# Second feed-forward product of an encoder layer: 26 block products on 4x4x2 blocks in place of one Strassen level

## The chip, the cores and the metric

One Trainium2 chip, one core. The metric is the device time of one execution in microseconds (us). The five engines that the text names are TensorE (PE), VectorE (DVE), ScalarE (ACT), GpSimd (POOL) and SyncE (SP). Here POOL and SP do little but issue transfers (DMA).

## The reference

One layer of a bidirectional encoder on x of 1024 tokens by 1024 channels. The first half (a gated mixing branch, a windowed attention branch, their merge) is untouched by the change. The second half is

```python
h2 = rmsnorm(x, norm2_g) * (1.0 + sc2) + sh2          # sc2, sh2, gt2: columns of silu(c) @ w_ada + b_ada
f_gate, f_up = jnp.split(h2 @ w_ffn_in, 2, axis=-1)   # w_ffn_in: 1024 x 5632
x = x + gt2 * ((jax.nn.silu(f_gate) * f_up) @ w_ffn_out)   # w_ffn_out: 2816 x 1024
```

All is fp32. The first feed-forward product is `h2 @ w_ffn_in`; the second is the hidden matrix (1024 tokens by 2816) times `w_ffn_out`.

## The kernel before

**Precision.** A matrix operand is split in two fp32r halves (`split2`: ACT casts it to the high half, DVE subtracts the high half from the value and writes the low half). A product of two operands is three matmuls: high by high, high by low, low by high.

**First feed-forward product.** The 2816 hidden columns are 22 tiles of 128, f = 0 to 21, in one level of Strassen: seven half-size products (STEPS, i = 0 to 6) of 12 matmuls for each f. The order is written out by hand: under `manual_schedule` each engine executes what is in the code, in the order in which it is in the code, and waits on semaphores. For f = 2 to 5 only i = 2 to 6 stand in the main loop (i = 0 and 1 came earlier); from f = 6 on all seven stand there. In one pass of the loop, `product(f, i)` issues the matmuls, `prepare(u + 2, 1)` works two weight units ahead (sums of weight blocks `ws` on DVE, cast on ACT, low half `wl` on DVE), and `evict(f, i)` combines the product in `xs`, `hs`, `t` or `t2`, applies silu on ACT and at i = 6 writes two tiles `hid` (minus the hidden values) of 128 x 512. PE waits for a low half if that is late.

**Sums for the second product.** `hidden_sums` forms four sums of hidden blocks for two f, one DVE operation a pass (`run_later`), and POOL stores the blocks in `tA`, `tB`; `load_out` loads `w_ffn_out` from f = 6 on, `out_sums` forms four weight sums and POOL stores them in `wS`.

**Second feed-forward product.** `work` has 77 units (seven Strassen products by 11 pairs of K tiles). A unit is [128 x 1024]: 512 columns of weights, 512 tokens of hidden values. SP loads it 12 units ahead in two transfers (`fetch`), `split_step` splits it four ahead, PE does 12 matmuls (`step_mm`). Units 0 to 2 use buffers of the first product's pool; the loads of later units wait until PE has read the last operand of the first product. Results are evicted by `finish`, `finish_rest` and `second_row` into accumulators `c1`, `e4`, `e7` and rows of x reloaded from DRAM (`x1d`). Within this stage eight columns of the gate gt2 are computed: SP loads 512 KB of `w_ada` and `ada_late` multiplies and reduces them in one DVE operation, written by the program as `raw<-raw,mid`. The last product's last row is done in two halves of 256 tokens.

All compute instructions carry the line of one helper (L144 before, L224 after); `dma` (SP) and `pool_dma` (POOL) are helpers too (L1265 and L1262).

Of the kernel before, what the change touches and what calls it, by code (L numbers as in the profile page):

```python
# [106 lines left out]
def kernel(  # L107
# [1816 lines left out]
    def hidden_tiles(f):  # L1924
        e, t = divmod(f, 2)
        if e not in hidden:
            hidden[e] = [mid.tile([P, 2048], F32, tag="mid", name=nm("hid"))]
        o = hidden[e][0]
        return [o[:, i * Q : (i + 1) * Q] for i in (2 * t, 2 * t + 1)]
# [29 lines left out]
    later = []  # L1959

    def run_later(n):
        for _ in range(n):
            if later:
                later.pop(0)()

    def hidden_sums(f):

        e, t = divmod(f, 2)
        if t == 0:
            hidden[e].append(mid.tile([P, 2048], F32, tag="mid", name=nm("hid")))  # L1970
        o, n = hidden[e]
        b = [o[:, i * Q : (i + 1) * Q] for i in range(4)]
        d = [n[:, i * Q : (i + 1) * Q] for i in range(4)]
        if t == 0:
            later.append(lambda: V.tensor_tensor(d[0], b[0], b[1], op=ALU.subtract))
            return
        pool_dma(tA[e], o)
        later.append(lambda: V.scalar_tensor_tensor(out=d[1], in0=d[0], scalar=-1.0, in1=b[3],
                                                    op0=ALU.mult, op1=ALU.subtract))
        later.append(lambda: V.tensor_tensor(d[2], b[3], b[1], op=ALU.subtract))  # L1980
        later.append(lambda: (V.scalar_tensor_tensor(out=d[3], in0=d[1], scalar=-1.0, in1=b[2],
                                                     op0=ALU.mult, op1=ALU.subtract),
                              pool_dma(tB[e], n)))

    wo_raw = {}

    def load_out(e):
        wo_raw[e] = mid.tile([P, 2048], F32, tag="mid", name=nm("wo"))
        for t in range(2):
            pool_dma(wo_raw[e][:, t * UNIT : (t + 1) * UNIT], w_out[2 * e + t])  # L1990

    def out_sums(e, part):

        w = wo_raw[e]
        a11, a21, a12, a22 = (w[:, i * Q : (i + 1) * Q] for i in range(4))
        out, a, b = ((a22, a21, a22), (a21, a11, a21), (a11, a22, a11), (a12, a11, a12))[part]
        V.tensor_tensor(out, a, b, op=ALU.add)
        if part == 3:
            pool_dma(wS[e], w)


# [90 lines left out]
    def out_row(e, t, d):  # L2092
        return w_out[2 * e + t][:, d * Q : (d + 1) * Q]

    def blk(x, i):
        return lambda e: x[e][:, i * Q : (i + 1) * Q]


    OUT = (
        (lambda e: out_row(e, 0, 0), blk(tA, 0), 1, True),  # L2100
        (lambda e: out_row(e, 1, 0), blk(tA, 2), 1, False),
        (blk(wS, 1), blk(tB, 2), 0, True),
        (lambda e: out_row(e, 1, 1), blk(tB, 3), 0, False),
        (blk(wS, 3), blk(tB, 0), 1, True),
        (blk(wS, 0), blk(tB, 1), 1, False),
        (blk(wS, 2), blk(tA, 3), 1, False),
    )
# [304 lines left out]
```

## Time and profile before

| | |
|---|---|
| median of 3 runs | 1211.98 us (1211.6 to 1212.04) |
| profiled execution | 1211.91 us, of which the span is 1210.1 us |
| PE busy | 1203.6 us (99%), 5632 matmuls |
| DVE busy | 924.0 us (76%) |
| ACT busy | 584.8 us (48%) |
| POOL busy | 155.4 us (13%) |
| DMA | 243.10 MB, mean 201 GB/s |
| first feed-forward product, main loop f = 2 to 5 | 637.50 to 691.91 us |
| f = 6 to 21 | 691.91 to 996.89 us |
| second feed-forward product | 996.89 us to the end |

Rows of the trace give start and duration in us, the engine, the operation and `out<-in` by tile names; a bracket at the end is the idle time before it and what ended it. The chain of waits is followed back from the last instruction, so engines on it set the end. DVE durations overlap a little at their ends: start to start of two neighbours is the pace. "us to landing" of a DMA counts from its issue to the arrival of its data.

### The profile page before, as it was taken

How to read it: one execution, taken by the hardware profiler on the slowest of the kernel's cores; microseconds unless marked ns; L12 is line 12 of the kernel's file. 1: busy time of each engine (PE TensorE's matmuls, PEld its weight loads, DVE VectorE, ACT ScalarE, POOL GpSimd, SP SyncE). 2: the span in 40 equal slices, each digit the busy share in tenths (PEclk: the TensorE clock that was granted, in tenths of full speed). 3: DMA queues.
4: the chain of work that ended last, by engine and by line, in shares of the span. 5: the costliest groups of instructions: out<-in, count | busy, mean ns of one | idle time of the engine just before them, and what ended most of it. 6: DMA issues, size and time to landing. Idle time of an engine off the chain costs nothing.

```text
span 1210.1 us, 15610 instructions
## 1 busy us (share of the span) xinstructions
PE 1203.6 (99%) x5632; PEld 1004.1 (83%) x5632; DVE 924.0 (76%) x1496; ACT 584.8 (48%) x958; POOL 155.4 (13%) x190
## 2 busy tenths in 40 slices
PE   9999999999999999999999999999999999999998
PEld 7888888888888888888888888888888888888887
DVE  9999967889978876898987757676676665765646
ACT  6668845367855443745553333333333334433341
POOL 0124323114322000011000000000000000000001
PEclk9999999999999999999999999999999999999999
DMA  9745169753177643567313545454555449995552
GB/s 372 283 157 192 35 228 318 289 226 122 71 273 266 213 150 100 172 222 266 104 61 118 187 175 208 182 201 158 181 207 191 157 168 380 393 344 191 193 173 105
DMA packets 80285, 243.10 MB, mean 201 GB/s; under 512 B 9168, under 2 KB 9424, under 8 KB 74960
## 3 DMA queue, kind: packets, MB, share of 16 engines
q1 hardware_dynamic: 64576, 167.65, 39.8%
q0 software_dynamic: 15632, 74.46, 16.2%
q8 instruction: 44, 0.72, 0.2%
q14 instruction: 33, 0.27, 0.1%
HBM read 180.73 MB, written 61.34 MB: 200 GB/s over the span
## 4 chain that ended last, share of the span: by engine, by line
PE 96%; DVE 2%; ACT 1%; DMA 0%; issue 0%; SPq 0%; DVEq 0%; ACTq 0%
PE mm L144 49%; PE at L144 47%; DVE mid L144 1%; ACT mid L144 0%; DVE wl L144 0%; DMA mid<-in_xA_dram 0%; DVE h L144 0%; ACT wh L144 0%; DVE lb L144 0%; ACT qhl L144 0%; DVE qhl L144 0%; ACT h L144 0%; DVE t L144 0%; SPq L201 0%; ACT kbuf L144 0%
## 5 line engine op out<-in xcount | busy, mean ns | idle before, releaser
L144 ACT CAST wh<-raw 128x1024 fp32r<-128x1024 f32 (+1 forms) x154 | 157.3, 1022 | 120.1 <-PE mm L144 39.5
L144 DVE TENSOR_TENSOR wl<-raw,wh 128x1024 fp32r<-128x1024 f32 (+1 forms) x141 | 165.2, 1175 | 61.4 <-ACT wh L144 60.5
L144 PE MATMUL mm<-mid,wh 128*128 128x512 f32 x640 | 197.3, 389 | 0.0
L144 PEld LDWEIGHTS mm<-mid,wh 128*128 128x128 f32 x640 | 119.9, 188 | 24.8
L144 PE MATMUL mm<-wh,h 128*128 128x512 f32 x384 | 124.6, 396 | 0.2 <-ACT h L144 0.2
L144 PE MATMUL mm<-mid,wl 128*128 128x512 f32 x320 | 124.5, 389 | 0.0
L144 PE MATMUL mm<-h,wh 128*128 128x512 f32 x304 | 94.3, 391 | 0.0
L144 PE MATMUL at<-h,wh 128*128 128x512 f32 x304 | 93.8, 390 | 0.0
L144 PEld LDWEIGHTS mm<-wh,h 128*128 128x128 f32 x384 | 70.7, 188 | 13.8 <-ACT h L144 0.4
L144 DVE TENSOR_TENSOR wl<-ws,wh 128x1024 fp32r<-128x1024 f32 (+1 forms) x50 | 55.9, 1117 | 24.4 <-ACT wh L144 24.4
L144 PE MATMUL mm<-wl,h 128*128 128x512 f32 x192 | 71.2, 391 | 0.0
L144 PEld LDWEIGHTS mm<-mid,wl 128*128 128x128 f32 x320 | 60.1, 188 | 12.4
L144 PEld LDWEIGHTS at<-h,wh 128*128 128x128 f32 x304 | 56.9, 188 | 11.7
L144 ACT CAST wh<-ws 128x1024 fp32r<-128x1024 f32 (+1 forms) x50 | 48.3, 966 | 37.3 <-DVE ws L144 24.9
L144 PEld LDWEIGHTS mm<-h,wh 128*128 128x128 f32 x304 | 56.6, 188 | 11.6
L144 ACT ACTIVATE t<-t 128x512 f32<-128x512 f32 x46 | 28.4, 630 | 70.8 <-DVE t L144 70.8
L144 DVE TENSOR_TENSOR ol<-raw,oh 128x1024 fp32r<-128x1024 f32 x30 | 36.6, 1223 | 31.1 <-ACT oh L144 29.4
L144 PE MATMUL at<-h,wl 128*128 128x512 f32 x152 | 59.3, 390 | 0.0
L144 PE MATMUL mm<-h,wl 128*128 128x512 f32 x152 | 59.2, 389 | 0.0
L144 ACT ACTIVATE xs<-xs 128x512 f32<-128x512 f32 x21 | 13.3, 632 | 94.0 <-DVE xs L144 94.0
L144 ACT CAST oh<-raw 128x1024 fp32r<-128x1024 f32 x30 | 31.7, 1055 | 44.4 <-PE at L144 21.6
L144 PE MATMUL at<-wl,wh 128*128 128x512 f32 (+1 forms) x136 | 52.7, 388 | 0.0
(302 smaller groups left out, 2871.0 us busy)
## 6 DMA issues: line engine op xcount, KB each, us to landing
mid<-in_w_ada_dram SPq DMA_DIRECT2D x30, 512.0 KB, 8.1
raw<-in_w_gate_dram SPq DMA_DIRECT2D x26, 512.0 KB, 3.8
tA<-hid POOLq DMA_DIRECT2D x11, 1024.0 KB, 4.6
tB<-hid POOLq DMA_DIRECT2D x11, 1024.0 KB, 5.2
wo<-in_w_out_dram POOLq DMA_DIRECT2D x22, 512.0 KB, 6.0
wS<-wo POOLq DMA_DIRECT2D x11, 1024.0 KB, 5.1
raw<-wS SPq DMA_DIRECT2D x44, 256.0 KB, 3.2
raw<-tB SPq DMA_DIRECT2D x44, 256.0 KB, 5.0
```

Of the source, the lines that this page charges most:

```text
L144: ins = f(*args, **kw)
```

## The change

The second product on the first 20 K tiles (five groups g of four tiles) uses 26 products of blocks (4 blocks of 256 weight columns, 4 K tiles, 2 halves of the tokens) where the plain product has 32; tiles 20 and 21 are done plainly (8 tail products). Each of the 130 units (26 products by 5 groups) is [128 x 768], 256 columns of weights and 512 tokens, with 6 matmuls; a tail product has 12.

- **Weight sums (A).** 28 sums of weight blocks (`A_OPS`), for two, two and one groups at a time: 84 DVE operations. Operands are loaded by SP in five registers of 128 x 512 (four in a tile `sums`, one `ss`) by a plan made by `registers`; results go by POOL to `pU` or `aX`, some come back later. 78 loads, 66 stores.
- **Token sums (B).** 18 sums of hidden blocks for each group: 90 DVE operations on eight registers (`hid` and the second `sums` tile), 14 loads and 18 stores a group. A group starts at f = 6, 8, 12, 16, 20. `evict` now stores the hidden tiles (`hR`, `hT`).
- **Place.** `run_sums(RATE)` issues 1.4 sums a pass from f = 2 on, in f = 2 to 5 all of them A.
- **gt2.** The eight `ada_late` and their loads (one buffer of 512 KB, in the second `sums` tile) move from the second product to the passes s = 0, 2, ... 16 of f = 2 to 5.
- **Second product.** `ORDER` gives the order of products, the bank pair and, for each result, the output rows and sign; DVE adds it straight to the row of x. A unit is split five ahead.
- **Removed.** `hidden_sums`, `out_sums`, `load_out`, `tA`, `tB`, `wS`, and the accumulators.

The diff, cut:

```diff
+NG = 5
+TAIL = 4 * NG
+UCOL = 768
+AHEAD_OF = 5
+RATE = 1.4
+A_OPS = (
+    (16, 0, 4, 1, -1), (17, 16, 2, 1, -1), (18, 17, 4, 1, 1), (19, 10, 2, -1, -1), (20, 11, 10, 1, -1),
...
+B_OPS = (
+    (8, 2, 6, 1, -1), (9, 3, 8, -1, 1), (10, 6, 9, 1, 1), (11, 0, 2, 1, 1), (12, 7, 9, 1, 1),
...
+    A_PLAN, B_PLAN = registers(A_ALL, 5, 3), registers(B_OPS, 8, 3)
...
+    def a_step(k):
+        (batch, v), _, _, ca, cb = A_ALL[k]
+        o, a, b = A_PLAN[1][k]
+        dst, n = a_place((batch, v))
+        w = slice(0, n * 256)
+        combine(a_regs[o][:, w], a_regs[a][:, w], a_regs[b][:, w], ca, cb)
+        if slot_of(A_OF, v) or (batch, v) in a_later:
+            pool_dma(dst, view(a_regs[o], dst, n))
+        a_loads(k)
...
+    def b_step(g, k):
+        v, _, _, ca, cb = B_OPS[k]
+        o, a, b = B_PLAN[1][k]
+        combine(b_regs[o], b_regs[a], b_regs[b], ca, cb)
+        for p in slot_of(B_OF, v):
+            pool_dma(pU[p, g][:, 256:], b_regs[o])
+        b_loads(g, k)
...
+    def gt2_step(n):
+        cond, raw = (gt2["m"][:, i * UNIT : (i + 1) * UNIT] for i in range(2))
+        if n > 0:
+            ada_late(raw, GT2 + n - 1, cond)
+        if n < 8:
+            dma(raw, w_ada2[GT2 - GT1 + n])
...
-            if i == 6:
-                hidden_sums(f)
-            elif f > 2:
-                run_later(1)
...
+                if s < 18 and s % 2 == 0:
+                    gt2_step(s // 2)
+                if i == 0 and f in (6, 8, 12, 16, 20):
+                    g = f // 4 - 1
+                    while b_queue:
+                        b_step(*b_queue.pop(0))
+                    b_loads(g, -1)
+                    b_queue.extend((g, k) for k in range(len(B_OPS)))
+                elif s:
+                    run_sums(RATE, 34 + 28 * max(0, (s - 6) // 28) - s)
...
-        for n in range(2, 4):
+        for n in range(2, AHEAD_OF):
             split_step(n)
...
+        def evict_out(k, x, sign, d, bank, cs=slice(0, Q)):
...
+            V.scalar_tensor_tensor(out=o, in0=bank[:, : cs.stop - cs.start], scalar=gt, in1=o,
+                                   op0=ALU.mult, op1=ALU.add)
```

**How DVE's order moves.** Three places, in DVE's program order. At the turn from f = 2 to f = 3, before (the two rows with `hid_1133` on the left are hidden sums):

```order
L144 TENSOR_TENSOR wl_1145_6309<-ws_1072_5753,wh_1144_6308 128x1024
L144 TENSOR_TENSOR wl_1151_6333<-ru_5754,wh_1150_6332 128x512
L144 TENSOR_TENSOR hid_1133_6203<-hid_1118_6062 128x512
L144 SCALAR_TENSOR_TENSOR hid_1133_6203<-hid_1133_6203,hid_1118_6062 128x512
L144 TENSOR_TENSOR ws_1072_5753<-ws_1072_5753 128x512
L144 TENSOR_TENSOR ws_1072_5753<-ws_1072_5753,raw_1130_6179 128x512
```

and now; a row that writes `sums_1140` or `ss_1141` is a weight sum, a row that writes `sums_1139,acc_mod_96` is one `ada_late`:

```order
L224 TENSOR_TENSOR wl_1147_6333<-ws_1072_5754,wh_1146_6332 128x1024
L224 SCALAR_TENSOR_TENSOR sums_1139_6249,acc_mod_96<-sums_1139_6249 128x1024
L224 TENSOR_TENSOR sums_1140_6250<-sums_1140_6250 128x512
L224 TENSOR_TENSOR wl_1151_6362<-ru_5755,wh_1150_6361 128x512
L224 SCALAR_TENSOR_TENSOR sums_1140_6250<-sums_1140_6250 128x512
L224 SCALAR_TENSOR_TENSOR sums_1139_6249,acc_mod_96<-sums_1139_6249 128x1024
L224 SCALAR_TENSOR_TENSOR sums_1140_6250<-sums_1140_6250 128x512
L224 TENSOR_TENSOR sums_1140_6250<-ss_1141_6251,sums_1140_6250 128x512
L224 TENSOR_TENSOR ws_1072_5754<-ws_1072_5754 128x512
L224 TENSOR_TENSOR ws_1072_5754<-ws_1072_5754,raw_1130_6180 128x512
```

Between the low half of a unit and the weight sums `ws` of the next one, two of the eight `ada_late` and four weight sums take the place of two hidden sums; between the two `ada_late` stand three operations.

The end of f = 5 and the start of f = 6, from the eviction of (5, 4) to the low half that the third product of f = 6 reads, before:

```order
L144 TENSOR_TENSOR xs_1175_6542<-mm_1108_5982,xs_1175_6542 128x512
L144 TENSOR_TENSOR wl_1177_6557<-raw_1147_6315,wh_1176_6556 128x1024
L144 TENSOR_TENSOR xs_1171_6521<-at_1174_6529,xs_1171_6521 128x512
L144 TENSOR_TENSOR ws_1072_5753<-ws_1072_5753 128x512
L144 TENSOR_TENSOR ws_1072_5753<-ws_1072_5753,raw_1147_6315 128x512
L144 SCALAR_TENSOR_TENSOR hid_1168_6502<-xs_1175_6542,xs_1171_6521 128x512
L144 SCALAR_TENSOR_TENSOR hid_1168_6502<-mm_1108_5982,hs_1109_5998 128x512
L144 TENSOR_TENSOR wl_1179_6590<-ws_1072_5753,wh_1178_6589 128x1024
```

and now:

```order
L224 TENSOR_TENSOR xs_1173_6611<-mm_1108_5983,xs_1173_6611 128x512
L224 TENSOR_TENSOR wl_1175_6635<-raw_1148_6340,wh_1174_6634 128x1024
L224 TENSOR_TENSOR sums_1140_6250<-sums_1140_6250 128x512
L224 TENSOR_TENSOR xs_1169_6587<-at_1172_6598,xs_1169_6587 128x512
L224 TENSOR_TENSOR sums_1140_6250<-sums_1140_6250 128x512 x2
L224 TENSOR_TENSOR ws_1072_5754<-ws_1072_5754 128x512
L224 TENSOR_TENSOR ws_1072_5754<-ws_1072_5754,raw_1148_6340 128x512
L224 SCALAR_TENSOR_TENSOR hid_1118_6063<-xs_1173_6611,xs_1169_6587 128x512
L224 SCALAR_TENSOR_TENSOR hid_1118_6063<-mm_1108_5983,hs_1109_5999 128x512
L224 TENSOR_TENSOR wl_1177_6675<-ws_1072_5754,wh_1176_6674 128x1024
```

Three weight sums (one row stands for two) came in between, ahead of the low half; the other added operations of f = 2 to 5 stand ahead of the first row shown.

The turn to the second product, from the low half of unit 0 on (`raw_1404` before, `raw_1378` now), before:

```order
L144 TENSOR_TENSOR wl_1444_8676<-raw_1404_8358,wh_1443_8675 128x1024
L144 TENSOR_TENSOR xs_1442_8659<-mm_1432_8587,xs_1442_8659 128x512
L144 TENSOR_TENSOR wo_1423_8511<-wo_1423_8511 128x512
L144 TENSOR_TENSOR xs_1438_8640<-at_1441_8646,xs_1438_8640 128x512
L144 TENSOR_TENSOR wl_1446_8697<-raw_1419_8486,wh_1445_8696 128x1024
L144 SCALAR_TENSOR_TENSOR hid_1430_8582<-xs_1442_8659,xs_1438_8640 128x512
L144 SCALAR_TENSOR_TENSOR hid_1430_8582<-mm_1432_8587,t2_1433_8600 128x512
L144 SCALAR_TENSOR_TENSOR hid_1431_8586<-hid_1431_8586,hid_1430_8582 128x512
L144 TENSOR_TENSOR hid_1431_8586<-hid_1430_8582 128x512
L144 SCALAR_TENSOR_TENSOR hid_1431_8586<-hid_1431_8586,hid_1430_8582 128x512
L144 TENSOR_TENSOR wl_1457_8751<-raw_1437_8622,wh_1456_8750 128x1024
L144 TENSOR_TENSOR ol_1459_8755<-raw2_1447_8723,oh_1458_8754 128x1024
```

and now (`hid_1118` and `sums_1139` on the left are registers of the token sums; the last two rows of a unit's split are `wl_1417` for unit 1, `wl_1430` for unit 2, `ol_1432` for unit 3):

```order
L224 TENSOR_TENSOR wl_1415_9040<-raw_1378_8685,wh_1414_9039 128x768
L224 TENSOR_TENSOR hs_1413_9021<-mm_1403_8943,hs_1413_9021 128x512
L224 TENSOR_TENSOR hid_1118_6063<-hid_1118_6063 128x512
L224 TENSOR_TENSOR hid_1118_6063<-sums_1139_6249,hid_1118_6063 128x512
L224 TENSOR_TENSOR xs_1409_9000<-at_1412_9008,xs_1409_9000 128x512
L224 TENSOR_TENSOR hid_1118_6063<-hid_1118_6063,sums_1139_6249 128x512
L224 TENSOR_TENSOR wl_1417_9065<-raw_1393_8827,wh_1416_9064 128x768
L224 SCALAR_TENSOR_TENSOR hs_1413_9021<-hs_1413_9021,xs_1409_9000 128x512
L224 SCALAR_TENSOR_TENSOR t2_1404_8956<-mm_1403_8943,t2_1404_8956 128x512
L224 TENSOR_TENSOR hid_1118_6063<-hid_1118_6063 128x512
L224 TENSOR_TENSOR wl_1430_9113<-raw_1408_8979,wh_1429_9112 128x768
L224 TENSOR_TENSOR ol_1432_9117<-raw2_1420_9094,oh_1431_9116 128x768
```

Four token sums, one of them (the third, which reads `sums_1139`) ahead of unit 1's low half with an operand that was stored and loaded again, replace one weight sum and three hidden sums, and the low halves of units 2 and 3 keep their place behind the last eviction.

More of the change, by code (lines that the diff above doesn't have):

```diff
@@ L573 @@
     EARLY = 6
+    A_ALL = [((b, o), (b, i), (b, j), ci, cj) for b in range(3) for o, i, j, ci, cj in A_OPS]
     firsts, raw2 = {}, []
@@ L1924, in hidden_tiles @@
     def hidden_tiles(f):
[L1925 to L1929, printed above, removed]
+        if not hidden:
+            hidden[0] = mid.tile([P, 2048], F32, tag="mid", name=nm("hid"))
+        return [hidden[0][:, i * Q : (i + 1) * Q] for i in (2 * (f % 2), 2 * (f % 2) + 1)]
     def evict(f, i):
         a, b, c = (banks.get((f, x)) for x in "abc")
-        e, t = divmod(f, 2)
         if i == 0:
@@ L1954, in evict @@
         else:
-            o = hidden_tiles(f)
+            o = hidden_tiles(f) if f < EARLY else (keep[f, "s"], keep[f, "c"])
             for t, x, y in ((o[1], keep[f, "c"], keep[f, "v"]), (o[0], a, keep[f, "s"])):
                 V.scalar_tensor_tensor(out=t, in0=x, scalar=-1.0, in1=y, op0=ALU.mult, op1=ALU.mult)
[L1959 to L1999, printed above, removed]
+        if i == 6:
+            for t in range(2):
+                pool_dma(hT[f - TAIL, t] if f >= TAIL else hR[2 * (f % 4) + t, f // 4], o[t])
@@ new lines, in b_loads, with run_sums @@
+    def b_loads(g, k):
+        for i, v in B_PLAN[0][k]:
+            dma(b_regs[i], b_place(g, v))
+    def b_step(g, k):
[5 more added lines that the diff above has]
+        b_loads(g, k)
+    a_queue = list(range(len(A_ALL)))
+    b_queue = []
+    credit, turn = [0.0], [0]
+    def run_sums(n, left=0):
+        credit[0] += n
+        while credit[0] >= 1 and (a_queue or b_queue):
+            credit[0] -= 1
+            turn[0] ^= 1
+            if b_queue and (turn[0] or not a_queue or len(b_queue) >= left):
+                b_step(*b_queue.pop(0))
+            elif a_queue:
+                a_step(a_queue.pop(0))
+            else:
+                b_step(*b_queue.pop(0))
+        credit[0] = min(credit[0], 1.0)
@@ L2089, in prepare @@
             n -= 1
[L2092 to L2107, printed above, removed]
[L2108 removed]
+    work = [(p, g) for _, p, _, _ in ORDER if p < NPROD for g in range(NG)]
     raws, ready = {}, {}
@@ L2272, with tail_load @@
-        ngt = sm(4, "ngt")
-        cond = midt(F32, 2)[:, 0, :]
-        gt2 = []
-        def step_mm(n, d, cs=slice(0, Q), out=None):
-            i, e = work[n]
-            _, _, b, first = OUT[i]
-            o = sets[b][d] if out is None else out
-            opens = first and e == 0 if out is None else e == NP - 2
+        ngt = sm(KT, "ngt")
+        V.tensor_scalar(ngt[:, :KT], mod[:, GT2 : GT2 + KT], -1.0, None, op0=ALU.mult)
+        tail_raw, tails = {}, {}
+        def tail_load(n):
+            r = wpool.tile([P, UNIT], F32, tag="raw", name=nm("raw"))
+            if n < 2:
+                dma(r, w_tail[n])
+            else:
+                dma(r.rearrange("p (t c) -> p t c", t=2), hT[n - 2].rearrange("t p c -> p t c"))
+            tail_raw[n] = r
```

316 lines of the change are left out of this document (197 added, 119 removed), and 17 rows, old and new, of tables (A_OPS, B_OPS, ORDER).

## Prediction

> **What bounds the kernel now.** I read the page first (busy times, then the chain), then the chain of waits from 640 us on, then busy times by stage.
>
> ```profile
> span 1210.1 us, 15610 instructions
> PE 1203.6 (99%) x5632; PEld 1004.1 (83%) x5632; DVE 924.0 (76%) x1496; ACT 584.8 (48%) x958; POOL 155.4 (13%) x190
> PE 96%; DVE 2%; ACT 1%; DMA 0%; issue 0%; SPq 0%; DVEq 0%; ACTq 0%
> ```
>
> TensorE is busy in 99% of the span and is 96% of the chain: the kernel is a line of matmuls, and whatever makes PE wait adds to the time. The profiled execution took 1211.91 us, 1.8 more than its span and 0.07 under the median, so sums below are made against 1211.9. In the chain by time, a row is a stretch of matmuls:
>
> ```profile
> 686.47 2.72 PE at L144 x12
> ...
> 691.91 38.08 PE at L144 x168
> ...
> 996.89 59.84 PE at L144 x264
> 1056.73 59.84 PE mm L144 x264
> 1116.57 89.14 PE at L144 x396
> ```
>
> No row of another engine stands in between, in the first product or the second. A matmul costs 59.84 / 264 = 0.2267 us, a product of 12 costs 2.72. Busy time by stage (columns: window, its length, then PE, PEld, DVE, ACT, POOL, the PE clock, DMA share, GB/s), for f = 2 to 5, its part from the eviction of (2, 4) to the low half of f = 6, f = 6, the second product, and its DMA-heavy part:
>
> ```profile
> 637.50:691.90 54.40, 54.40 (x242) 45.05 (x241) 38.96 (x55) 18.15 (x25) 2.19 (x4) 1.00 0.44 155
> 645.80:693.80 48.00, 48.00 (x214) 39.73 (x213) 34.91 (x48) 14.89 (x21) 2.27 (x5) 1.00 0.43 153
> 691.91:710.95 19.04, 19.04 (x86) 15.77 (x85) 11.85 (x16) 6.53 (x10) 2.13 (x4) 1.00 0.60 221
> 996.89:1195.00 198.11, 198.11 (x876) 164.04 (x875) 124.70 (x133) 83.28 (x83) 7.70 (x13) 1.00 0.73 261
> 1030.00:1060.00 30.00, 30.00 (x134) 24.82 (x134) 22.76 (x28) 11.70 (x12) 3.81 (x7) 1.00 1.04 395
> ```
>
> DVE has 13 us to spare in the 48 us of the second row. That is the slack the change must live on in f = 2 to 5, since all that it adds there goes to DVE and to transfers. The last row shows transfers at 395 GB/s with a share of 1: I take that as what they can carry.
>
> The DVE rows give prices:
>
> ```profile
> 645.78 0.69 DVE L144 TENSOR_TENSOR xs<-mm,xs 128x512 f32<-128x512 f32 x1 [1.09 <-PE mm L144]
> 646.39 1.22 DVE L144 TENSOR_TENSOR wl<-ws,wh 128x1024 fp32r<-128x1024 f32 x1
> ...
> 691.95 0.69 DVE L144 SCALAR_TENSOR_TENSOR hid<-mm,hs 128x512 f32<-128x512 f32 x1
> 692.56 1.22 DVE L144 TENSOR_TENSOR wl<-ws,wh 128x1024 fp32r<-128x1024 f32 x1
> ...
> 998.89 0.68 DVE L144 SCALAR_TENSOR_TENSOR hid<-hid,hid 128x512 f32<-128x512 f32 x1
> 999.49 0.68 DVE L144 TENSOR_TENSOR hid<-hid 128x512 f32<-128x512 f32 x1
> ...
> 1000.69 1.21 DVE L144 TENSOR_TENSOR wl<-raw,wh 128x1024 fp32r<-128x1024 f32 x1
> 1001.83 1.21 DVE L144 TENSOR_TENSOR ol<-raw,oh 128x1024 fp32r<-128x1024 f32 x1
> ...
> 1048.12 1.22 DVE L144 SCALAR_TENSOR_TENSOR raw<-raw,mid 128x1024 f32<-128x1024 f32 x1
> 1049.26 0.08 DVE L144 DVE_READ_ACCUMULATOR raw<-raw,mid 128x1 f32 x1
> 1054.73 2.79 DVE L144 SCALAR_TENSOR_TENSOR mid<-at,mod,mid 128x512 f32<-128x512 f32 x4
> ```
>
> Start to start a 512-wide operation costs 0.60 (998.89 to 999.49), a 1024-wide one 1.14 (1000.69 to 1001.83), so 0.87 for 768; an `ada_late` 1.22 with its accumulator read; an eviction added to a row 2.79 / 4 = 0.70. The low half of the third product of f = 6 starts at 692.56 and ends at 693.8; PE needs it at 691.91 + 2 x 2.72 = 697.35. So it is 3.5 us early now.
>
> Transfers (out<-in, KB, median us to landing, each from the DMA view; the second row is the total of f = 2 to 5, from its window):
>
> ```profile
> raw<-in_w_ada_dram SPq DMA_DIRECT2D x8, 512.0 KB, 6.6
> DMA packets 1731, 8.43 MB, mean 153 GB/s; under 512 B 192, under 2 KB 192, under 8 KB 1216
> raw<-in_w_gate_dram SPq DMA_DIRECT2D x4, 512.0 KB, 4.4
> ru<-in_w_up_dram SPq DMA_DIRECT2D x2, 512.0 KB, 3.4
> out_dram<-mid POOLq DMA_DIRECT2D x12, 256.0 KB, 2.6
> x1d<-mid POOLq DMA_DIRECT2D x12, 256.0 KB, 3.8
> pd<-t POOLq DMA_DIRECT2D x24, 256.0 KB, 4.8
> hs<-pd SPq DMA_DIRECT2D x12, 256.0 KB, 2.6
> raw<-in_w_out_dram SPq DMA_DIRECT2D x5, 256.0 KB, 3.5
> raw<-tA SPq DMA_DIRECT2D x33, 256.0 KB, 5.4
> ```
>
> A 256 KB store by POOL takes 2.6 to 4.8 (middle row 3.8), a 256 KB load 2.6 to 5.4 (I take 3.8, near 3.5), a 512 KB load 3.4 to 6.6 (I take 4.4).
>
> **The change part by part.**
>
> *Matmuls.* 77 x 12 = 924 now, 130 x 6 + 8 x 12 = 876 then: 48 fewer at 0.2267, **-10.9 us**. The last row is cut in halves as before: 0.
>
> *f = 2 to 5, DVE work.* From the eviction that starts at 645.78 to the low half at 692.56 (included), DVE's program has 73 operations: 24 weight sums, 8 `ada_late`, 8 low halves of 1024, two tiny ones (0.1 each) and 31 others of 512. Work: 55 x 0.60 + 8 x 1.14 + 8 x 1.22 + 0.2 = 52.1. Add 1.5 for casts that low halves still wait for, an estimate from waits such as this one, most of which the sums would fill:
>
> ```profile
> 668.61 0.69 DVE L144 TENSOR_TENSOR wl<-ws,wh 128x512 fp32r<-128x512 f32 x1 [1.66 <-ACT wh L144]
> ```
>
> From 645.78 that ends at 699.4; PE needs it at 697.35: **2.0** late even if no operand is ever late.
>
> *f = 2 to 5, DVE waits for operands.* DVE is in order: an operation that waits for a load holds up evictions and low halves behind it. With one buffer, an `ada_late` load is issued when the one before has read it. Twice only three 512-wide operations stand between two (front part, first place): 4.4 - 1.8 = 2.6 each, ends 1.6 and 4.8. With five registers, five times a result is stored and its register loaded again for use three sums on, or a register is loaded for use two or three sums on. By counting the operations in between: sum 8 to 11 has 6.6 us of cover against store and load 3.8 + 3.8 = 7.6, so 1.0 is waited; 11 to 14 a load, 3.8 against 2.95: 0.85; 12 to 15, 7.6 against 5.3 and the 0.85: 1.45; 19 to 21 a load, 3.8 against 1.85: 1.95; 19 to 22, 7.6 against 4.2 and the 1.95: 1.45; 20 to 23, 7.6 against 3.45 and the last two: 0.75. Together 5.2 + 7.45 = 12.65. With 2.6 for each 256 KB transfer and 3.4 for 512 KB it is 3.2 + 1.75 = 4.95; with 4.8, 5.4 and 6.6, where more of the gaps are short, about 23. Work and waits add, since DVE has no idle time left: 2.0 + 12.65 = **+14.7**, ends 7 and 25.
>
> A second count gives a floor that needs no order: 8.43 MB, less 4.19 of removed stores, plus 4.7 (gt2), 28 loads and 20 stores of sums (12.6) and 8 hidden tiles (2.1) is 23.6 MB; at 395 GB/s that is 60 us for a stage of 54.4, 5.6 late. Loads would then be nearer their long ends.
>
> *f = 6 to 21.* Token sums at 1.4 a pass of 2.72 are 1.94 us apart, so three sums give 5.8 of cover against 7.6 for a store and a reload. DVE gets 9.8 sums in 19.04 us where it had about 4.8: 11.85 + 3.0 of 19.04, not full. Such a wait, 1.8, in front of a low half that is some 3.3 early is covered; in f = 6 and 7, where all sums are token sums, two fall close together and pass it by 1 to 2. From f = 8 on the two kinds alternate and cover doubles: 0. **+2**, ends 0 and 8.
>
> *Turn to the second product.* The third unit's load is the first that waits for PE, as now:
>
> ```profile
> 994.20 0.33 SPq L1265 DMA_DIRECT2D raw<-in_w_out_dram  x1
> ```
>
> Its low half `ol` comes at 1001.83 in the row above, 4.9 us after the stage's start at 996.89. PE needs unit 3 after three units of 2.72, at 8.2; with 6 matmuls a unit it needs it at 4.1. A 768-wide half is 0.3 shorter; so 0.5 to 1 late. Ahead of unit 1's low half stands a token sum whose operand is stored, then loaded (7.6) with 3.2 us of work in between, 4.4 waited; it began about 7 us before the stage, so it ends near 0.7 and pushes the low halves of units 1 and 2 to about 2.2 and 4.5, needed at 1.4 and 2.7. **+3**, ends 0.5 and 8 with the new loads of x on POOL.
>
> *Second product.* DVE: 130 x 0.87 + 4 x 1.14 + 60 x 0.70 = 160 us of 876 x 0.2267 = 198.6, 80%, where it had 124.7 of 198.1; the cast on ACT is narrower in proportion. Transfers: 130 x 393 KB = 51 MB and some 8 MB of x, tails and output, 59 MB in 198.6 us, 297 GB/s under 395, 12 units ahead. **0**, ends 0 and +6.
>
> Sum: -10.9 + 14.7 + 2 + 3 + 0 = +8.8, 1211.9 + 8.8 = **1221 us**. All low ends give -10.9 + 7 + 0 + 0.5 = -3.4, 1208.5; all high ends -10.9 + 25 + 8 + 8 + 6 = +36, 1248.
>
> [...]
>
> **Rivals.**
> 1. *No operand is late* (faster side). Then -10.9, the 2.0 of DVE's work and up to 2 at the turn remain: 1203 to 1205, or 1201 if the casts cost nothing. For it: no stage of before shows PE waiting on DVE, POOL is at 13%. Against: 60 us of transfers are due in 54.4. It decides if a store and a reload stay under 4.2 to 6.6 together, the covers above, and a load of 512 KB under 1.8; the shortest rows are 2.6, 2.6 and 3.4.
> 2. *Short transfers*, stores and loads at 2.6: -3.4 to 0, 1208.5 to 1212, on the border of no change. For it: nothing but these transfers runs on POOL then. Against: of the rows above only `out_dram` and `hs` are that short.
> 3. *Transfers full*: f = 2 to 5 and f = 6 to 7 at the long ends (+25, +8) and a second product short of data (+6): 1211.9 - 10.9 + 39 = 1240. For it: the count of 23.6 MB. Against: f = 2 to 6 are now at a share of 0.60 or less, and 12 units are loaded ahead in the second product.
>
> **How the numbers follow.** Forecast (waits as counted, 1214.5 to 1232): 0.52; rival 1: 0.20; rival 2: 0.15; rival 3: 0.13. A measurement of this kernel can tell 0.2% from no change, 2.4 us: 1209.6 to 1214.4. Faster takes rival 1 and a third of rival 2, 0.25; same most of the rest of it and an edge of the forecast, 0.13; slower 0.62. The range cuts about a tenth at each end, half of rival 1 below and the far part of rival 3 above: 1203 to 1239; the forecast's own is 1214 to 1232.
>
> **What would show it.** Right: PE idle in 640 to 715 us of the new trace, ended by DVE `wl`, of 8 us or more; DVE rows in f = 2 to 5 with idle time ended by DMA into `sums` or `ss`; DMA share near 1 there; PE without gaps from f = 8 to 20; one gap of some us at the turn; matmuls 5593 (48 fewer, and 15 cut in halves where 6 were). Wrong: DVE idle in f = 2 to 5 ended by PE as now; stores that land in 2.6 and loads in 2.6 under load; a gap-free chain there (rival 1); or idle PE spread through the second product, ended by loads of units (rival 3).

## The result and the profile after

The changed kernel takes 1272.34 us (median of 4 runs, 1268.76 to 1274.77), the kernel before 1211.91: a ratio of 1.0497, 95% interval 1.0471 to 1.0522. The forecast was 1221 us, 1203 to 1239: the direction was right, the size wrong by 51 us. The profiled execution (1274.77 us) has a span 62.9 us longer than before. Its page:

```profile
span 1273.0 us, 16590 instructions
PE 1215.2 (95%) x5593; PEld 1006.4 (79%) x5593; DVE 1013.0 (80%) x1660; ACT 609.8 (48%) x1007; POOL 247.1 (19%) x342
...
PEclk9999999999999999999988889999999999899999
...
PE 72%; DMA 10%; DVE 7%; issue 6%; POOL 2%; ACT 1%; SPq 1%; POOLq 0%; DVEq 0%; ACTq 0%
```

PE has the 5593 matmuls foretold, yet it is busy 11.6 us longer, where 48 fewer should make it 10.9 shorter: 22.5 us more than it should be. About 17 of them are half of the 34.9 us that PE computed in the stretches in which the trace records a granted clock of 0.50 (most lie in the row of 8s, about 635 to 765 us); the other 5 are not resolved further. The rest is idle time, 57.8 us where 6.5 were: 51.3 more. 22.5 - 10.9 + 51.3 = 62.9, the whole difference. The chain is no longer a line of matmuls.

Busy time by stage (columns as in the prediction), for f = 2 to 5, f = 6 and 7, f = 8 to 21, the turn, and the second product after it:

```profile
637.50:727.50 90.00, 62.36 (x242) 49.27 (x241) 55.73 (x85) 17.14 (x24) 18.47 (x28) 0.85 0.72 247
727.50:775.00 47.50, 41.73 (x169) 33.05 (x168) 31.94 (x45) 12.60 (x19) 11.75 (x21) 0.93 0.75 258
775.00:1056.67 281.67, 272.78 (x1177) 223.90 (x1176) 210.28 (x312) 91.34 (x127) 84.05 (x147) 0.98 0.77 262
1056.67:1100.00 43.33, 33.92 (x130) 25.55 (x129) 30.57 (x37) 23.16 (x28) 6.46 (x10) 0.92 1.03 383
1100.00:1250.00 150.00, 150.00 (x664) 124.31 (x663) 124.82 (x149) 84.02 (x101) 5.83 (x10) 1.00 0.87 288
```

f = 2 to 5 took 54.4 us and takes 90.0 (+35.6), f = 6 and 7 47.5 for 38.1 (+9.4), f = 8 to 21 281.7 for 266.9 (+14.8); the second product with the end 216.3 for 213.2 (+3.1, where -10.9 was due, so 14.0 lost). The sum is +62.9.

In f = 2 to 5 PE pauses four times, each time at the last product of an f, until VectorE has evicted product 4, whose bank it writes (brackets: idle time before, and what ended it):

```profile
655.22 1.22 PE L224 MATMUL mm<-mid,wh 128*128 128x512 f32 x2 [6.52 <-DVE xs L224]
682.56 1.22 PE L224 MATMUL mm<-mid,wh 128*128 128x512 f32 x2 [11.96 <-DVE xs L224]
701.22 0.73 PE L224 MATMUL mm<-mid,wh 128*128 128x512 f32 x2 [3.33 <-DVE xs L224]
722.95 1.22 PE L224 MATMUL mm<-mid,wh 128*128 128x512 f32 x2 [5.78 <-DVE xs L224]
```

Two matmuls take 0.62 us at full clock (the pair at 643.10); after three of these pauses they take 1.22, and the granted clock is 0.50 there (651.54 to 658.36, 675.43 to 685.67, 719.80 to 726.63). What VectorE did in the second pause, and SP's queue at that time:

```profile
672.94 1.22 DVE L224 SCALAR_TENSOR_TENSOR sums<-sums 128x1024 f32<-128x1024 f32 x1 [5.86 <-DMA sums<-in_w_ada_dram]
...
679.88 0.69 DVE L224 TENSOR_TENSOR sums<-ss,sums 128x512 f32<-128x512 f32 x1 [5.10 <-DMA pU<-sums]
...
681.82 0.68 DVE L224 TENSOR_TENSOR xs<-mm,xs 128x512 f32<-128x512 f32 x1
```

```profile
665.30 0.33 SPq L1346 DMA_DIRECT2D sums<-in_w_ada_dram  x1
```

The eviction `xs<-mm` stands behind two waits. An `ada_late` waits 5.86 for a load that was issued at 665.30 and landed at 672.9 (7.6 us); then a sum waits 5.10 for a register whose store has to land first. VectorE's waits of f = 2 to 5, grouped (us in total, times, longest):

```profile
DVE sums L224 <- DMA sums<-in_w_blk_dram: 10.4, 2, 8.9
DVE sums L224 <- DMA sums<-in_w_ada_dram: 9.7, 3, 5.9
DVE sums L224 <- DMA pU<-sums: 5.1, 1, 5.1
DVE sums L224 <- DMA sums<-pU: 3.6, 3, 2.8
DVE wl L224 <- ACT wh L224: 2.8, 4, 1.2
DVE ss L224 <- DMA sums<-pU: 1.2, 1, 1.2
DVE ss L224 <- DMA ss<-in_w_blk_dram: 1.1, 1, 1.1
```

The waits for transfers are 31.1 us of this, against 12.65 in the prediction. With VectorE's work, 55.7 in the row of the stage above, and 2.8 for casts they make 89.6 of the 90.0 us, and none of VectorE's waits there is ended by PE. So VectorE's own row, work plus waits, sets the length of f = 2 to 5, and PE's pauses and its half clock both lie inside that length. In f = 6 and 7 it is much the same: 31.7 of work, 13.6 of waits for transfers and 1.2 for a cast are 46.5 of 47.5. From f = 8 on it is not.

The transfers are not much slower than the rows of before; the loads' and stores' medians there are

```profile
sums<-in_w_ada_dram SPq DMA_DIRECT2D x8, 512.0 KB, 5.2
pU<-sums POOLq DMA_DIRECT2D x14, 256.0 KB, 4.4
sums<-pU SPq DMA_DIRECT2D x6, 256.0 KB, 4.5
```

so a store and a reload take 8.9 where I took 7.6, and the stage's transfers ran at 247 GB/s.

### The profile page after: what moved, and what is told of

Same layout as the page of the kernel before. It is cut to its first block, busy times and chain, and to the rows that moved or that the text cites. A ratio compares the mean times of both kernels' runs of the same rounds, so it can differ in the third digit from the quotient of the medians.

```text
span 1273.0 us, 16590 instructions
## 1 busy us (share of the span) xinstructions
PE 1215.2 (95%) x5593; PEld 1006.4 (79%) x5593; DVE 1013.0 (80%) x1660; ACT 609.8 (48%) x1007; POOL 247.1 (19%) x342
## 4 chain that ended last, share of the span: by engine, by line
PE 72%; DMA 10%; DVE 7%; issue 6%; POOL 2%; ACT 1%; SPq 1%; POOLq 0%; DVEq 0%; ACTq 0%
PE mm L224 43%; PE at L224 29%; DMA pU<-sums 3%; DVE ws L224 2%; DMA raw<-in_w_tail_dram 1%; DVE wl L224 1%; DVE mid L224 1%; DVE hid L224 1%; DMA hid<-hR 1%; POOL pU L1343 1%; DMA sums<-pU 1%; DVE sums L224 1%; DMA pU<-hid 1%; POOL hR L1343 1%; DMA sums<-hR 1%
## 5 line engine op out<-in xcount | busy, mean ns | idle before, releaser
L224 PE MATMUL mm<-mid,wh 128*128 128x512 f32 x640 | 204.0, 401 | 31.0 <-DVE xs L224 27.6
L224 ACT CAST wh<-raw 128x1024 fp32r<-128x1024 f32 (+2 forms) x164 | 155.4, 950 | 85.8 <-PE mm L224 37.7
L224 DVE TENSOR_TENSOR wl<-raw,wh 128x1024 fp32r<-128x1024 f32 (+2 forms) x151 | 161.6, 1077 | 35.6 <-ACT wh L224 35.0
L224 PEld LDWEIGHTS mm<-mid,wh 128*128 128x128 f32 x640 | 122.9, 194 | 59.1 <-DVE xs L224 29.3
L224 PE MATMUL mm<-mid,wl 128*128 128x512 f32 x320 | 127.4, 398 | 0.1
L224 ACT CAST oh<-raw 128x768 fp32r<-128x768 f32 x73 | 61.2, 839 | 51.8 <-PE mm L224 20.2
L224 DVE TENSOR_TENSOR ol<-raw,oh 128x768 fp32r<-128x768 f32 x73 | 68.3, 954 | 14.2 <-ACT oh L224 13.9
L1343 POOL DMA_DIRECT2D pU<-sums x73 | 45.9, 629 | 117.5 <-DVE sums L224 116.8
L224 DVE TENSOR_TENSOR wl<-ws,wh 128x1024 fp32r<-128x1024 f32 (+1 forms) x50 | 55.9, 1117 | 15.4 <-ACT wh L224 15.4
L224 PEld LDWEIGHTS mm<-h,wh 128*128 128x128 f32 x304 | 56.7, 188 | 11.6
L1343 POOL DMA_DIRECT2D pU<-hid x70 | 38.3, 548 | 129.5 <-DVE hid L224 128.0
```

Source lines behind the costliest of these rows:

```text
L224: ins = f(*args, **kw)
L1343: nc.gpsimd.dma_start(dst, src)
```

## The experiments

Length of each stage in all runs, in us (f = 2 to 5 from 637.5; "second" is from its first matmul to the end of the span), and the time of the run (for runs made four times the median, with the stages of the profiled one; all but the changed kernel, e7_combined, e11_best and e15_best ran once). Where no row of a stage was edited, it scatters: f = 2 to 5 from 88.8 to 91.1, f = 6 to 21 from 315.5 to 329.2, the second product from 216 to 218. So a difference of less than 14 us in f = 6 to 21 tells nothing.

```
run                     total    f 2-5   f 6-21   second
before                 1211.9     54.4    305.0    213.2
changed                1272.3     90.0    329.2    216.3
e1_ada_once            1264.7     80.6    326.8    218.0
e2_sums_no_transfer    1248.9     72.7    319.4    217.5
e3_no_transfer         1238.2     66.5    315.5    216.9
e8_pool_loads          1268.4     93.7    318.7    216.8
e9_narrow              1248.0     80.0    312.1    216.6
e10_no_transfer_all    1224.4     67.4    304.6    213.1
e5_sums_late           1262.1     62.7    342.9    217.2
e7_combined            1268.4     55.7    337.1    232.9
e11_best               1234.5     55.4    322.7    219.8
e15_best               1239.7     55.6    320.9    224.1
e6_turn                1276.6     90.8    330.0    216.5
e12_depth              1275.0     91.1    324.6    220.0
e13_half_bytes         1260.2     88.8    322.7    209.5
e14_tails_late         1264.8     89.2    317.8    218.5
```

### VectorE's work or its waits

```diff
-        if n < 8:
+        if n == 0:
             dma(raw, w_ada2[GT2 - GT1 + n])
```

> The changed kernel with one load of w_ada in place of eight; the eight multiply-and-reduce operations stay and work on the same data (gt2 is then not that of the reference). Changed kernel: f = 2 to 5 loses 35.6 us (gaps of PE 27.6, half clock 8.0). Theory 1 (VectorE stands in its order at operands that have not landed, evictions wait behind, PE waits for a bank): the 9.7 us of VectorE waits that end with a w_ada load go, and with them 9 to 14 us of the total, 1258 to 1263. Rival A (VectorE simply has too many operations there): no change, 1268 to 1275.

1264.7 us, a little over the 1258 to 1263 expected; f = 2 to 5 lost 26.2 in place of 35.6. The loads of w_ada are a quarter of it.

```diff
         for i, v in A_PLAN[0][k]:
-            src, n = a_place(v)
-            dma(view(a_regs[i], src, n), src)
+            if v[0] > 0:
+                src, n = a_place(v)
+                dma(view(a_regs[i], src, n), src)
...
-        if slot_of(A_OF, v) or (batch, v) in a_later:
+        if batch and (slot_of(A_OF, v) or (batch, v) in a_later):
...
```

> The changed kernel with the 28 weight sums of f = 2 to 5 working on registers loaded once: no loads and no stores for them, all VectorE operations stay (the second product reads raw weight blocks for groups 0 and 1, so the output is not the reference's). Theory 1: the waits on operands and stores of sums, some 20 us in f = 2 to 5, go; the w_ada waits stay; total 1245 to 1255. Rival A: no change in f = 2 to 5, total 1268 to 1275. Rival C (transfers as such are at their limit): like theory 1, but the w_ada waits go too, total under 1245.

1248.9 us, f = 2 to 5 lost 18.3: the operands of the sums are half of it.

> Both edits at once: VectorE has every operation of the changed kernel in f = 2 to 5 and none of the added transfers. Theory 1: f = 2 to 5 loses 0 to 5 us (the work alone, 2 by the prediction's count), total 1234 to 1242. Rival A: f = 2 to 5 still loses over 20 us, total over 1258.

1238.2 us, f = 2 to 5 lost 12.1. More than the 0 to 5 expected; the largest pause left is the first:

```profile
654.15 1.22 PE L224 MATMUL mm<-mid,wh 128*128 128x512 f32 x2 [5.62 <-DVE xs L224]
670.46 0.73 PE L224 MATMUL mm<-mid,wh 128*128 128x512 f32 x2 [1.04 <-DVE xs L224]
686.02 0.73 PE L224 MATMUL mm<-mid,wh 128*128 128x512 f32 x2 [1.05 <-DVE xs L224]
701.16 0.73 PE L224 MATMUL mm<-mid,wh 128*128 128x512 f32 x2 [0.83 <-DVE xs L224]
```

It belongs to the first sum, which waits for the loads that fill the registers (the 8.9 in the groups above). The other three, some 1 us each, are VectorE's work: 2.9 us in pauses, and 4.1 of the stage's 12.1, since its only wait for a transfer is 8.0 us long; the prediction had 2.0. In all these runs the stage is as long as VectorE's row: it waits 31.1 us for transfers in the changed kernel, 21.7, 12.4 and 8.0 in the three runs, and the stage less these waits is 58.6 to 60.4 us in all four. With all sums of the kernel free of transfers,

```diff
...
-        if slot_of(A_OF, v) or (batch, v) in a_later:
-            pool_dma(dst, view(a_regs[o], dst, n))
-        a_loads(k)
...
-        for i, v in B_PLAN[0][k]:
-            dma(b_regs[i], b_place(g, v))
+        for i in range(8) if k < 0 and g == 0 else ():
+            dma(b_regs[i], w_blk[i][:, :Q])
...
-        for p in slot_of(B_OF, v):
-            pool_dma(pU[p, g][:, 256:], b_regs[o])
...
```

> The changed kernel with no load and no store for any sum, weight or token, and one w_ada load; all VectorE operations stay on registers loaded once (the second product reads raw blocks; the output is not the reference's). VectorE's work alone: f = 2 to 5 as in the run without transfers there (12.1, of which a 5.6 us wait for the first load), f = 6 to 21 loses 0 to 2 in place of 24.2, the second product as now. Theory 1: 1212 - 10.9 + 12 + 1 + 14 = 1226 to 1230. Rival A (work): f = 6 to 21 keeps over 8 us of loss, over 1234.

it took 1224.4 us, and f = 6 to 21 lost nothing, though VectorE did every operation of the change there:

```profile
704.90:1009.50 304.60, 304.60 (x1345) 252.32 (x1344) 241.44 (x359) 105.34 (x146) 18.59 (x34) 1.00 0.27 88
```

Rival A, too much work, falls for f = 6 to 21 and has about 4 of 35.6 us in f = 2 to 5. This run also shows what half clock is worth where VectorE sets the length: f = 2 to 5 had 10.2 us of it, e3_no_transfer 3.4, and the stage took 67.4 us for 66.5, a difference that the first wait explains alone (8.8 for 8.0).

### Queue, registers, or transfers as such

```diff
-            dma(view(a_regs[i], src, n), src)
+            pool_dma(view(a_regs[i], src, n), src)
```

> The changed kernel with the loads of weight-sum operands issued on POOL's queue in place of SP's, so that no w_gate, w_up or w_ada load stands behind a load that waits for a store. Theory 1a (the order of SP's queue makes the waits): 10 to 20 us less, 1252 to 1262. Theory 1b (store and reload of one register is the wait, whatever queue): within 5 us of 1272.

1268.4 us, and f = 2 to 5 even 3.7 longer. VectorE's waits for w_ada there fell from 9.7 to 6.0 us, its other waits for transfers rose from 21.4 to 27.3: behind POOL's stores the loads are no earlier. So in f = 2 to 5 the order of SP's queue alone is not the cause; a queue for these loads alone was not tried. From f = 6 on it has a part, which SP's waits from 727 to 745 in the changed kernel show:

```profile
SPq L1346 <- DMA pU<-ss: 9.9, 2, 5.5
```

The first loads of token sums were issued at 739.0, behind a load of a weight sum's operand that stood in SP's queue until a store had landed, and VectorE waited 6.3 us for them.

Then the registers:

```diff
-    A_ALL = [((b, o), (b, i), (b, j), ci, cj) for b in range(3) for o, i, j, ci, cj in A_OPS]
+    A_ALL = [((b, o), (b, i), (b, j), ci, cj) for b in range(NG) for o, i, j, ci, cj in A_OPS]
...
-    A_PLAN, B_PLAN = registers(A_ALL, 5, 3), registers(B_OPS, 8, 3)
+    A_PLAN, B_PLAN = registers(A_ALL, 10, 6), registers(B_OPS, 8, 3)
...
-        g, n = 2 * batch, min(2, NG - 2 * batch)
+        g, n = batch, 1
...
```

> The changed kernel with weight sums for one group at a time: 140 operations of 256 columns in place of 56 of 512 and 28 of 256 (0.34 us each, the same VectorE time), ten registers of 256 in the same space in place of five, operands loaded six sums ahead in place of three, transfers of 128 KB, twice as many. Place and pace as in the changed kernel. Theory 1 (few registers, so a store and a reload lie inside three sums): f = 2 to 5 loses 12 to 22 us in place of 35.6 (w_ada's buffer and the first loads remain), total 1250 to 1260. Rival D (number or volume of transfers): f = 2 to 5 loses as much or more, 1270 or more.

1248.0 us: 21 to 27 us less than the four runs of the changed kernel, from the same space. f = 2 to 5 lost 25.6 (12 to 22 were expected), 10 less; f = 6 to 21 lost 7, where runs in which it was not edited lost 10.5 to 24. The gain is not that of the number of registers alone: in f = 2 to 5 this run formed 41 narrow sums, as many columns as 20.5 wide ones where the changed kernel has 24, and the smaller transfers landed sooner (stores 3.9 us for 4.4, loads 4.1 for 4.3).

Next the place. `run_sums` now takes the weight sums and the token sums of a pass as two numbers:

```diff
...
-                    run_sums(RATE, 34 + 28 * max(0, (s - 6) // 28) - s)
+                    run_sums(*((0, 0) if f < EARLY else (0, RATE) if f < 8 or f >= 20 else (1.02, 0.75)))
...
```

> The changed kernel with the 84 weight sums spread over f = 8 to 19 at 1.02 a pass, token sums there at 0.75 a pass, none of the weight sums in f = 2 to 5; the w_ada columns stay in f = 2 to 5 with their one buffer. Theory 1 (a late operand costs only where VectorE and the banks have no slack; spread out, store plus reload has 8 us and is covered): f = 2 to 5 loses 0 to 5 us in place of 35.6, f = 8 to 21 no more than its 14.8 now, total 1235 to 1245. Rival D (the sums cost the same wherever they stand, since transfers are short of room everywhere): total 1260 to 1275.

1262.1 us: a miss. f = 2 to 5 fell to +8.3, but f = 6 to 21 rose to +37.9. The total lies in rival D's range. It is no proof of it, as e15_best below shows; that five wide registers at one sum a pass still leave a store and a reload inside three sums is my reading, which no run tested by itself.

The same with three buffers and a later start of the token sums, and the turn's edits (below):

```diff
...
+        three = (gt2["m"][:, UNIT:], gt2["a"][:, :UNIT], gt2["a"][:, UNIT:])
         if n > 0:
-            ada_late(raw, GT2 + n - 1, cond)
-        if n < 8:
-            dma(raw, w_ada2[GT2 - GT1 + n])
+            ada_late(three[(n - 1) % 3], GT2 + n - 1, cond)
+        for m in range(3) if n == 0 else (n + 2,):
+            if m < 8:
+                dma(three[m % 3], w_ada2[GT2 - GT1 + m])
...
+                    run_sums(*((0, 0) if f < EARLY or f in (6, 8, 12, 16, 20) and i < 3 else
+                               (0, 1.75) if f < 8 or f >= 20 else (1.02, 0.8)))
...
```

> Weight sums in f = 8 to 19 as in the run with late sums, no sum in the first three passes of a token group, three buffers for the w_ada loads (the registers of the weight sums are free then), the turn's casts and evictions as in the run on the turn. Theory 1: f = 2 to 5 loses 0 to 2, f = 6 to 21 0 to 8, the turn 2 to 6: 1212 - 10.9 + 2 to 16 = 1203 to 1217, full clock nearly throughout. Rival D: over 1235.

1268.36 us (ratio 1.0478, 1.0456 to 1.0499). Three w_ada buffers and no sums bring f = 2 to 5 to 55.7, 1.3 over before. But f = 6 to 21 lost 32, where 0 to 8 were expected, much as in e5_sums_late. And my pace left eight weight sums over, which then stood between the low halves of units 1 and 2 at the turn and made PE pause 15.4 us; the run tells nothing of the turn.

That, with the tail's casts where they were in the changed kernel, the narrow sums of e9_narrow, 7 units ahead, and this pace:

```diff
...
+                    run_sums(*((0, 0) if f < EARLY else
+                               (0, 0 if f in (6, 20) and i < 2 else 1.6) if f < 8 or f >= 20 else
+                               (1.7, 0 if f in (8, 12, 16) and i < 3 else 0.8)))
...
```

> All remedies together: narrow weight sums with ten registers, in f = 8 to 19 only; three w_ada buffers; the first token sums of a group two or three passes behind their loads; evictions ahead of the next split; units loaded 7 ahead. Theory 1 and 3: f = 2 to 5 loses 0 to 2, f = 6 to 21 5 to 15, the second product gains 3 to 10: 1212 - 10 + 5 to 17 = 1205 to 1220. Rival D (transfers as such): f = 6 to 21 loses over 25, total over 1235.

1234.51 us (ratio 1.0179, 1.0162 to 1.0196), the fastest complete version, still 22.6 us slower than before and outside the 1205 to 1220 expected. f = 6 to 21 lost 17.7 with 1.7 narrow sums a pass.

And slower over a longer way, 12 units ahead, with the tails late (as in e14_tails_late):

```diff
...
+                    run_sums(*((0, 0) if f < EARLY else (0, 0) if f == 6 and i < 2 else
+                               (1.3, 0 if f in (8, 12, 16, 20) and i < 2 else 1.6 if f < 8 or f >= 20 else 0.75)))
...
```

> Narrow weight sums with ten registers at 1.3 a pass over f = 6 to 21, three w_ada buffers, token sums two passes behind their loads, evictions ahead of the next split, tails late, units loaded 12 ahead. Theory 1 with what was measured so far: f = 2 to 5 loses 1, f = 6 to 21 8 to 16 (17.8 with 1.7 a pass over f = 8 to 19), second product 207 to 212 in place of 213.4: 1212 + 1 + 12 - 4 = 1214 to 1224.

1239.66 us (ratio 1.0225, 1.0208 to 1.0242), again outside the 1214 to 1224 expected: f = 6 to 21 lost 16, as foreseen, but the second product took 224.1. Two windows of it, from f = 9 into f = 20 and the turn:

```profile
760.30:988.80 228.50, 228.50 (x1010) 189.20 (x1009) 187.90 (x317) 78.25 (x108) 87.80 (x164) 1.00 0.85 290
1014.00:1060.00 46.00, 36.09 (x140) 25.07 (x139) 33.58 (x47) 22.54 (x28) 10.61 (x17) 1.00 0.98 362
```

For 228.5 us, with both kinds of sums, VectorE at 82% and transfers at a share of 0.85, PE never stops. So there neither the sums nor their bytes cost anything: rival D falls. All of this run's loss of 16 us in f = 6 to 21 lies before 760 and after 989. Before 760 PE paused 6.17 us; VectorE had waited 5.73 for a token sum's operand, whose load was issued at 729.7, behind a weight sum's load that stood 6.4 us in SP's queue until a store had landed. So here, as at f = 6 of the changed kernel, the order of SP's queue is part of it.

### The clock

```diff
+        scratch = ss_tile()
+        DOSE = {8: 6, 11: 8, 14: 10, 17: 13}
...
+            if i == 4 and f in DOSE:
+                d = scratch[:, :Q]
+                for k in range(DOSE[f]):
+                    x = d if k else ws[:, :Q]
+                    V.tensor_tensor(d, x, x, op=ALU.subtract)
             if not copies:
                 evict(f, i)
```

> The kernel before with 6, 8, 10 and 13 idle subtractions of 512 columns on VectorE ahead of the eviction of product 4 at f = 8, 11, 14 and 17, which should make PE pause about 1, 2, 3.5 and 5 us there. Theory 2 (a pause of about 2.6 us or more halves PE's clock for some us): the two long pauses are followed by matmuls at half clock, 1.7 us or more lost each on top of the pause, the short ones are not; total 1212 + 11.5 + 3.5 to 7 = 1227 to 1231. Rival (the low clock of the changed kernel comes from its transfers or VectorE load): pauses cost themselves alone, 1222 to 1225, clock 1.00 throughout.

1224.59 us, 12.55 more than the run of before beside it. The total lies in the rival's range, but only because the pauses came out shorter than planned, 0, 0.71, 2.16 and 4.34 us, so the clock has to decide:

```profile
804.63 0.73 PE L144 MATMUL mm<-mid,wh 128*128 128x512 f32 x2 [0.71 <-DVE xs L144]
864.21 0.73 PE L144 MATMUL mm<-mid,wh 128*128 128x512 f32 x2 [2.16 <-DVE xs L144]
927.58 1.22 PE L144 MATMUL mm<-mid,wh 128*128 128x512 f32 x2 [4.34 <-DVE xs L144]
```

```profile
800.00:812.00 12.00, 11.29 (x50) 9.03 (x49) 11.76 (x18) 2.33 (x4) 2.13 (x4) 1.00 0.30 117
860.00:872.00 12.00, 9.84 (x37) 7.62 (x36) 11.80 (x17) 2.09 (x3) 0.00 (x0) 0.86 0.18 74
923.00:940.00 17.00, 12.66 (x44) 10.01 (x43) 14.56 (x21) 3.58 (x5) 0.55 (x1) 0.80 0.31 99
```

The granted clock (the column behind POOL's) stays at 1.00 around 0.71, is 0.86 over 12 us around 2.16 and 0.80 over 17 us around 4.34: half speed for 2 x 0.14 x 12 = 3.4 and 2 x 0.20 x 17 = 6.8 us. The pauses add up to 7.2 us, and PE's busy time rose by 5.1, half of 3.4 + 6.8. So in a kernel with none of the change's transfers the clock fell behind a pause alone: theory 2 stands, and its low end is at 2.16 us or below. PE sets the time in this kernel, and pauses and half clock together, 7.2 + 5.1, are nearly all of its 12.55; in f = 2 to 5 of the changed kernel, where VectorE sets the length, the 8.0 us that half clock adds to PE's busy time (62.4 for 54.4) lie inside VectorE's 89.6.

### The turn

```diff
-                    run_sums(RATE, 34 + 28 * max(0, (s - 6) // 28) - s)
+                    run_sums(RATE if f < 20 else 1.7, 34 + 28 * max(0, (s - 6) // 28) - s)
...
-            if n in (8, 10, 12, 14):
-                tail_split(n // 2 - 4)
+            if n in (12, 14, 16, 18):
+                tail_split(n // 2 - 6)
...
+                    flush()
                     after_unit(n)
-                    flush()
```

> The changed kernel with three edits at the turn: the casts of the plain tail four units later (n = 12, 14, 16, 18), evictions ahead of the next split in VectorE's order, and 1.7 sums a pass in f = 20 and 21. Now the second product loses 14.0 us (gaps 9.4, half clock 4.6). If those gaps are what the rows say (a cast of the tail that waits for its load with unit casts behind it, an eviction behind a split, low halves behind the last token sum): the loss falls to 2 to 6, total 1260 to 1266. Rival (the units' own loads are late at the start, 385 GB/s): no change, 1269 to 1274.

1276.6 us, second product 216.5. In the changed kernel PE's first two pauses of the stage, 1.31 and 1.02 us, stand behind the last token sums; here they are gone, PE pauses for the first time 19 us into the stage, and the stage is as long as in the changed kernel (216.3). So neither the last token sums nor the order of casts and evictions is it alone.

```diff
-        for n in range(3, 12):
+        for n in range(3, 7):
             fetch(n)
...
-            fetch(n + 12)
+            fetch(n + 7)
```

> The changed kernel with the second product's units loaded 7 ahead in place of 12. Theory 3 (at the turn transfers are full, 385 GB/s; with 12 units, x rows and the tail in flight together, each waits for all): the second product's 216.3 us fall to 203 to 210, total 1259 to 1266. Rival (bytes, not their order, are short, or 7 is too shallow): 214 or more, total 1270 or more.

1275.0 us, second product 220.0: 7 units ahead are worse, not better.

```diff
+        if 3 < n < 80 and n % 2:
+            raws[n] = raws[n - 1]
+            return
...
```

> The changed kernel; in the second product every odd unit from 5 to 79 is not loaded but split again from the buffer of the unit before it: half the bytes, every split, matmul and eviction as before (the output is not the reference's). Second product now 216.3 us, of which about 14 are lost in its first 40. Theory 3b (transfers are full at the turn, so units, tail and x rows arrive late): 203 to 207. Rival (the order of casts and low halves behind the last token sums): 213 or more.

1260.2 us, second product 209.5, between the two answers: 6.8 of the 14.0 us hang on the bytes left out. That is a lower bound for the transfers, since they still ran at 361 GB/s in the first 40 us. Of the pauses left, 1.9 us stand behind the last token sum and 3.6 behind ACT's casts, which waited longest for the tail:

```profile
ACT tail L224 <- DMA raw<-in_w_tail_dram: 6.1, 2, 3.6
ACT tail L224 <- DMA raw<-hT: 3.4, 1, 3.4
...
ACT oh L224 <- DMA raw<-pU: 2.3, 2, 1.3
```

```diff
...
+    for c, p, rows in ((0, 24, (6, 0, 2, 5)), (1, 12, (1, 3, 4, 7))):
+        j = next(j for j, e in enumerate(out) if e[1] == p) + 1
+        out[j:j] = [(c, NPROD + x, ((x, 1),), 1) for x in rows]
```

> The changed kernel with all eight plain tail products behind the units 75 and 80 in place of among the first 27 products, on bank pairs of their own (16 evictions more), their loads at units 52 to 58 and casts at 64 to 70. Theory 3b: 2 MB less in the first 25 us, no cast of a late load in front of units: second product 207 to 212. Rival (the tails only show a shortage that is there anyway): 214 or more.

1264.8 us, second product 218.5. Counted as time less 0.2267 us for each matmul, 12.2 us are lost in the first 60 us of the stage, where the changed kernel loses 14.2; the late tails then cost 4.2 more. So at most some 2 us hang on the tails' place at the turn, no more than this stage scatters, and in e15_best, too, some 7 of the 22 us lost by this count stand at the late tails.

None of these runs shows the turn without full transfers: in the first 40 us of the second product they moved 357 to 384 GB/s in all of them. But full transfers alone don't stop PE. Before, the same 40 us had

```profile
996.89:1036.89 40.00, 40.00 (x179) 33.10 (x178) 23.63 (x24) 19.92 (x21) 1.07 (x2) 1.00 1.02 378
```

with no pause. What changed is how long a unit lasts and what comes between: 512 KB were enough for 2.72 us of matmuls, now 384 KB for 1.36. The loads of the first 25 us, before (996 to 1021; the other half of a unit, `tA`, took 6.2)

```profile
raw<-in_w_out_dram SPq DMA_DIRECT2D x13, 256.0 KB, 6.1
...
mid<-x1d SPq DMA_DIRECT2D x2, 256.0 KB, 6.1
```

and now (1055 to 1080):

```profile
raw<-pU SPq DMA_DIRECT2D x12, 384.0 KB, 9.9
mid<-x1d POOLq DMA_DIRECT2D x6, 512.0 KB, 13.3
raw<-in_w_tail_dram SPq DMA_DIRECT2D x2, 512.0 KB, 14.4
```

The rows of x are 3.1 MB of these 25 us, where they were 0.5. That units, rows of x and tails together ask for more than comes is what the rows show; how the 14.0 us divide among them stays open, and no run moved the rows of x.

## Why the prediction was wrong

Against the forecast of 1220.7 the profiled execution took 54 us more: 20.9 in f = 2 to 5, 22.2 in f = 6 to 21 and 11.0 in the second product.

**Right.** The direction; operands that land late in front of evictions as the mechanism; the rule for f = 2 to 5, "work and waits add, since DVE has no idle time left": there VectorE's work and waits fill 89.6 of 90.0 us. VectorE's work cost about 4 us there, where 2.0 were counted. That f = 6 to 21 loses nothing without late operands, as in rival 1, is shown by e10_no_transfer_all; its total, 1224.4, is still far from rival 1's 1203 to 1205, since the first fill and the turn stayed.

**The step that failed first: the waits of f = 2 to 5, 12.65, measured 31.1.** Three things are in the difference. The first sum's 8.9 us stood in no term: I counted loads that come back, not those that fill the registers at the start. Waits for w_ada were 9.7, not 5.2, since such a load took up to 7.6. The waits for sums' operands and stores were 12.5, not 7.45, with 8.9 for store and reload. Put into the same sum, the measured waits and work give nearly all of the 35.6 us.

**f = 6 to 21, +2, measured +24.2** (10.5 to 24 in the runs that left it as it was). The cover I counted (5.8 us, or twice that from f = 8) was held against 7.6; here a store and a reload take 8.3 to 9.1 (4.0 for a store, 4.3 or 5.1 for a load). The first loads of the token sums, and a queue in which they stand behind a load that waits for a store, were in no term (6.3 us waited at f = 6 alone). And f = 6 and 7 were counted with time to spare on VectorE, whose work and waits filled them.

**Turn and second product, +3 and 0, measured 14.0.** The token sum ahead of unit 1 did wait, 3.2 us for the 4.4 counted, and PE paused 2.3 us behind it: that part was right. But 297 GB/s under 395 was a mean over a stage that has its peak, 384 GB/s, in the first 40 us. I took the prefetch as cover; at the turn it is itself the load. Here the mechanism of rival 3 was at work, which had 6 us for it.

**No term for the clock.** I had read the clock column of before, 1.00 throughout, as if it would stay. Matmuls at half clock are most of 22.5 us of PE's time, but not all of that is in the miss: about 12 lie in f = 2 to 7, where VectorE's row sets the length and PE would have waited anyway. Some 10 us, in f = 8 to 21 and at the turn, can have added to the time. The shortest pause with half clock behind it was 2.63 us in the changed kernel (at 783.25) and 2.16 in e4_gap_dose.

No run here is a version that beats the kernel before: e10_no_transfer_all, with no transfer for any sum, still took 213.1 us for the second product, as before's 213.2. What the matmuls saved was spent at its start.
